# TensorE's order where phases follow each other: from the scheduler's choice to an order by counts of passed columns

## The chip, the core and the metric

The kernel runs on one NeuronCore of one Trainium2 chip. The metric is the device time of one execution in microseconds (us), as the median of several executions. A core has five engines that run their own instruction queues side by side: TensorE (PE: matmuls, with PEld for its weight loads), VectorE (DVE), ScalarE (ACT), GpSimd (POOL) and SyncE (SP, which here only issues DMAs). They meet through semaphores.

## What is computed

A decoder of two layers over 1040 tokens (16 meta tokens and 1024 real ones), 1024 features wide, in float32. Every sub-layer stands between two RMS norms:

```
def rmsnorm(x, g):                      # over the features
    return x * rsqrt(mean(x * x) + EPS) * g

def conv_ffn(x, w_up, conv_w, w_down):
    gate, val = split(causal_dwconv(x @ w_up, conv_w))
    return (silu(gate) * val) @ w_down

for l in range(2):
    hn = rmsnorm(h, g[0])
    mix = hgrn2_mixer(hn) if l == 0 else fox_mixer(hn, *shared_kv(h))
    h = h + rmsnorm(mix, g[1])
    h = h + rmsnorm(conv_ffn(rmsnorm(h, g[2])), g[3])
return h[:, 16:]
```

So at four places a product must be finished for all 1024 features before its tokens can be normalised, added to the stream, normalised again and used by the next product: after the mixer of layer 0, after its feed-forward part, after the mixer of layer 1, and after the last feed-forward part, which ends the kernel. These four places are called the **joins** here.

## The kernel before

Features lie on partitions and tokens on columns. The tokens are cut into three blocks (`BLK_A`: 356, 342, 342 columns; `BLK_B`: 342 each), and the 1024 features into eight tiles of 128 (`KT`). A float32 product is made of float32r parts, high and low: for each tile of the contracted dimension `mm3s` (line 141) issues three matmuls (lines 145, 148, 149) of 342 or 356 columns and yields the number of columns passed, 1026 or 1068. Such three matmuls are called a **pair** in this document (a pair of weight tile and input tile). `mm3` runs `mm3s` without stopping.

The program is written with a framework that has a scheduler: it places the instructions of each engine by priority (the order of the text, shifted by `tc.high_priority(offset=...)`) and by its own idea of when operands are ready, and draws all semaphores. Inside `tc.manual_schedule(engines={PE})` TensorE's instructions stay in the order of the text. Before the change this holds for the two woven stages (lines 543, 711, 1031), not for the joins.

A join is written by `overlap(blocks, work, done, then)` (line 218). `work(acc, i, sl)` makes row tile `i` of a block: four pairs into a PSUM bank, an evacuation by DVE (line 575 or 681) and `sumsq`, which squares the tile on ACT and adds the square to `acc` on POOL (lines 187, 188). Eight row tiles, 32 pairs, make a block. `done` is `post` (line 191) for the finished block:

- `rstd_of` (line 156): six small matmuls at line 164 sum `acc` over the features (called **S** here), ACT takes the root (line 169), DVE the reciprocal and a diagonal (lines 170, 175), and six matmuls at line 176 spread it over the partitions (called **R**).
- the **gain loop** over the eight tiles: a load of the residual by DMA, a multiplication (line 207) and an addition (line 208) on DVE, a store by DMA, and where another norm follows `split_gain` (ACT line 280 or 97, DVE line 281 or 98) and the squares of the new stream, added on POOL (line 188).
- a second `rstd_of` for the norm that follows (called **PS**, its sums, and **PR**, its root), whose result ACT copies into `r` (line 179). The last join has none.

`then(b)` is the next phase's first work on block `b`: at the first and third join three hidden tiles, five times eight pairs, each with a convolution on DVE and ACT (lines 607 to 614, `high_priority`); at the second the projections k, v, q (eight pairs each) and the forget logits z (`zf`, line 736, 16 matmuls) of the first head pair.

The text before the change puts S and R of a block behind the first row tile of the next block (`LAG` 1), PS and PR of the block before it just ahead of them, the last block's S and R behind the first step of `then(0)` (`LAG2` 1); the scheduler then moves TensorE's instructions as it sees fit. Tiles have few buffers: `pj` (products) 2, `pd` (statistics) 2, `po` 1, `acc` 2, `rstd` (the diagonal) 1.

Of the kernel before, what the change touches and what calls it, by code (L numbers as in the profile page):

```python
# [20 lines left out]
KT = D // P  # L21
# [9 lines left out]
BLK_A = [(0, 356), (356, 342), (698, 342)]  # L31
# [7 lines left out]

OFF, OFF_W0, OFF_W = 1000, 0, 300  # L40

LAG, LAG2 = 1, 1


AHEAD, RUSH, SLACK = 2, 2, 5000
# [10 lines left out]
def tile_yoco(ctx: ExitStack, tc: tile.TileContext, hT, gains, lbl, w_in, head_g, w_oa,  # L56
# [92 lines left out]
            PE.matmul(pt, wl, xh[:, sl], start=False, stop=(j == n - 1))  # L149
            yield (2 + (xl is not None)) * pt.shape[-1]  # L150

    def mm3(pt, pairs, sl):
        for _ in mm3s(pt, pairs, sl):
            pass

    def rstd_of(accs, r=None):


        n = accs[0].shape[-1]
        cs = [slice(c, min(c + QR, n)) for c in range(0, n, QR)]  # L160
        pt = psum("pd")
        for j, c in enumerate(cs):
            for i, acc in enumerate(accs):
                PE.matmul(pt[:c.stop - c.start, j:j + 1], acc[:, c], ones[:, :1], start=(i == 0), stop=(i == len(accs) - 1))
        q = sm.tile([P, 4], F32, tag="rq", name=nm("rq"), bufs=2)
        m = cs[-1].stop - cs[-1].start
        k = len(cs) - (m < QR)
        for rows, j in ((QR, slice(0, k)), (m, slice(k, len(cs))))[:1 + (m < QR)]:
            A.activation(q[:rows, j], pt[:rows, j], AF.Sqrt, bias=eps[:rows])
            V.reciprocal(q[:rows, j], q[:rows, j])  # L170
        dg = tmp("rstd", n)
        pr = psum("pd")[:, :n]
        for j, c in enumerate(cs):
            m = c.stop - c.start
            V.tensor_scalar(dg[:m, c], ident[:m, :m], q[:m, j:j + 1], float(D), ALU.mult, ALU.mult)
            PE.matmul(pr[:, c], ones[:m], dg[:m, c], start=True, stop=True)
        if r is None:
            return pr
        A.copy(r, pr)
# [11 lines left out]
    def post(acc, m, sl, gpost, res, keep, pre=None, more=None):  # L191


        n = sl.stop - sl.start
        r1 = rstd_of([acc])
        acc = None
        for kt in range(KT):
            mk = m[kt][:, sl]
            if more is None or kt % 4 < 2:
                rs = tmp("res", n)  # L200
            elif isinstance(more, int):
                ru = unit(more, "res") if kt % 2 == 0 else ru
                rs = ru[:, (kt % 2) * 350:][:, :n]
            else:
                rs = tmp(more[kt % 2], n)
            nc.sync.dma_start(rs, res[kt][:, sl])
            V.scalar_tensor_tensor(mk, mk, gsb[:, gpost, kt:kt + 1], r1, ALU.mult, ALU.mult)
            V.tensor_add(mk, mk, rs)  # L208
            dst = keep(kt, sl)
            nc.sync.dma_start(dst, mk[:, n - dst.shape[-1]:])  # L210
            if pre is not None:
                split_gain(pre[1][kt], mk, pre[0], kt, sl)
                acc = sumsq(acc, mk, "sq2")
        yield
        if pre is not None:
            rstd_of([acc], pre[2][:, sl])

    def overlap(blocks, work, done, then=None):


        def row_tiles(b):
            t0, n = blocks[b]
            acc = None
            for i in range(KT):
                acc = work(acc, i, slice(t0, t0 + n))
                yield
            behind.append(done(acc, slice(t0, t0 + n)))

        def some(g, k=99):
            while k and next(g, g) is not g:  # L230
                k -= 1

        behind = []
        nb = len(blocks)
        for b in range(nb):
            g = row_tiles(b)
            some(g, LAG)
            if b:
                if b > 1:
                    next(behind[b - 2], None)  # L240
                next(behind[b - 1])
            some(g)
        g = then(0) if then else iter(())
        some(g, LAG2)
        next(behind[nb - 1])
        next(behind[nb - 2], None)
        some(g)
        for b in range(1, nb):
            g = then(b) if then else iter(())
            if b == nb - 1:  # L250
                next(behind[b], None)
            some(g)

    def weave(a, wa, b, wb, lead):

# [43 lines left out]
    def norm0(i):  # L299
        sl = slice(BLK_A[i][0], BLK_A[i][0] + BLK_A[i][1])  # L300
        accs = [None, None]
        for kt in range(KT):
            accs[kt % 2] = sumsq(accs[kt % 2], x0[kt][:, sl], eng=V if i == 0 and kt % 2 else G)
        rstd_of(accs, r0[:, sl])

    w0 = [W.cols(w_in, [D])]
    take(0)
# [238 lines left out]
    def mixer_out(o, w, blocks, WW, mix, done, then):  # L546


        mx = [None] * KT

        def part(kts):
            x = []
            for kt in kts:
                *ou, src = o(kt)
                split(*(t[:, blocks[0][0]:] for t in (*ou, src)))
                x.append((WW.rows(w, kt * P), ou))
            return x

        def one():
            x = part(range(4))  # L560
            for ot in range(KT):
                mx[ot] = unit(mix[ot], f"mix{ot}")
                for t0, n in blocks:
                    pt, sl = psum("pj")[:, :n], slice(t0, t0 + n)
                    yield from mm3s(pt, [(wt(ot), ou) for wt, ou in x], sl)
                    A.copy(mx[ot][:, sl], pt)

        def two():
            x = part(range(4, 8))

            def work(acc, ot, sl):
                pt = psum("pj")[:, :sl.stop - sl.start]
                mm3(pt, [(wt(ot), ou) for wt, ou in x], sl)
                with tc.high_priority(offset=OFF):
                    V.tensor_add(mx[ot][:, sl], mx[ot][:, sl], pt)
                    return sumsq(acc, mx[ot][:, sl])

            overlap(blocks, work, lambda acc, sl: done(acc, mx, sl), then)

        return one, two  # L580
# [16 lines left out]
    def ffn(l, blocks, x, r, WW, hid, accu, done, then=None):  # L597
# [22 lines left out]
        def tile_up(j):  # L620
            c0, m = HID[j]

            ua, ub = hid[count["hid"] % len(hid)]
            hh, hl = unit(ua, f"h{j}", F32R), unit(ub, f"h{j}", F32R) if m == P else None
            count["hid"] += 1
            ws = [WW.cols(w_up[l], [c0]), WW.cols(w_up[l], [DFF + c0])] if m == P else [WW.cols(w_up[l], [c0, DFF + c0])]
            halo = [None, None]

            def block(t0, n):
                sl, y = slice(t0, t0 + n), []  # L630
                for i, w in enumerate(ws):
                    if i:
                        yield
                    pt = psum("pj")[:, :n]
                    mm3(pt, [(w(kt), x[kt]) for kt in range(KT)], sl)
                    with tc.high_priority(offset=OFF):
                        yi, halo[i] = conv(pt, j + i * FT, halo[i], sl)
                    y.append(yi)
                if m < P:
                    y.append(tmp("y", n))  # L640
                    A.copy(y[1][:m], y[0][m:2 * m])
                yg, yv = y[0][:m], y[1][:m]
                A.activation(yg, yg, AF.Silu)
                V.tensor_mul(yv, yv, yg)
                if m == P:
                    split(hh[:, sl], hl[:, sl], yv)
                else:
                    A.copy(hh[:m, sl], yv)
                    V.tensor_sub(hh[m:, sl], yv, f(hh[:m, sl]))
                yield  # L650

            return (hh, hl), block

# [18 lines left out]
        def downs(ci, hs, ws):  # L672

            def down(ot, sl):
                pt = psum("g")[:, :sl.stop - sl.start]
                mm3(pt, [(w(ot), h_) for w, h_ in zip(ws, hs)], sl)
                with tc.high_priority(offset=OFF):
                    if ci == 0:
                        A.copy(acc_u[ot][:, sl], pt)
                    else:  # L680
                        V.tensor_add(acc_u[ot][:, sl], acc_u[ot][:, sl], pt)  # L681

            def work(acc, ot, sl):
                down(ot, sl)
                with tc.high_priority(offset=OFF):
                    return sumsq(acc, acc_u[ot][:, sl])

# [3 lines left out]
            for ot in range(KT):  # L691
                if ci == 0:
                    acc_u[ot] = unit(accu[ot], f"acc{ot}")
                for t0, n in blocks:
                    down(ot, slice(t0, t0 + n))

        count = {"hid": 0, "halo": 0}
        return first, rest
# [301 lines left out]
    def heads0(i):  # L1000
# [3 lines left out]
        for which in ("zkvq" if i == NB - 1 else "kvqz"):  # L1004
            if which == "z":
                zf(i, *zs)
                forget(i, *zs)
            else:
                for _ in project(which, 0, i):
                    pass  # L1010
            yield
        if i:
            turn(0, i - 1)
        if i == NB - 1:
# [61 lines left out]
```

## Time and profile before

| | us |
|---|---|
| median of three runs | 2878.49 (2877.14 to 2882.29) |
| the profiled execution, its own time | 2883.05 |
| its span, first to last instruction | 2881.1 |
| TensorE busy / DVE busy / ACT busy / POOL busy | 2768.6 / 1830.8 / 1258.2 / 369.6 |
| TensorE's mean granted clock | 0.982 of full |

The table's engine times are sums over the span. All numbers of the trace come from the profiled execution, which is 4.6 us above the median. A granted clock of 1.00 is 2.4 GHz; the other level that the rows show is half of it, and a stretch between the two had both.

### The profile page before, as it was taken

The page shows a single profiled execution, that of the slowest core. Times are in us where ns is not written, and L with a number is a line of the kernel's source. Part 1 is how long each engine was busy: PE and PEld are TensorE (multiplying, and loading weights), DVE is VectorE, ACT ScalarE, POOL GpSimd, SP SyncE. Part 2 cuts the span into 40 slices and gives each one's busy share as a digit, 9 for nine tenths or more (in the row PEclk, how much of TensorE's full clock was granted, in tenths as well). Part 3 has the DMA queues.
Part 4 walks back from the last instruction along what each step waited for, and adds up shares of the span by engine and source line. Part 5 has one row for each costly group of instructions (what it writes and reads, how often), then busy time and mean ns, then how long its engine had stood idle before and what let it go on. Part 6 is the DMA issues. An engine that isn't in the chain of part 4 may idle for free. (4 is left out here: it accounts for less than half of the span.)

```text
span 2881.1 us, 45581 instructions
## 1 busy us (share of the span) xinstructions
PE 2768.6 (96%) x17706; PEld 2709.2 (94%) x17706; DVE 1830.8 (64%) x3737; ACT 1258.2 (44%) x2421; POOL 369.6 (13%) x741
## 2 busy tenths in 40 slices
PE   8999999989999999999889999999989999999997
PEld 8999999989999999999789988898989999999997
DVE  5545445285655655566878888887684665565566
ACT  6445445455322322233566666666555232232232
POOL 2000000041100000004400000000240100010012
PEclk9999999999999999999899999999999999999999
DMA  4111111142211111112311111112242111121103
GB/s 132 30 38 30 38 40 49 37 125 62 66 38 52 45 52 38 44 52 67 92 45 45 45 45 45 45 45 93 70 124 59 45 52 52 30 65 39 52 30 113
DMA packets 202921, 163.14 MB, mean 57 GB/s; under 512 B 13984, under 2 KB 194128, under 8 KB 202704
## 3 DMA queue, kind: packets, MB, share of 16 engines
q1 hardware_dynamic: 202704, 160.23, 19.2%
q8 instruction: 138, 2.26, 0.3%
q14 instruction: 79, 0.65, 0.1%
HBM read 139.53 MB, written 20.66 MB: 56 GB/s over the span
## 5 line engine op out<-in xcount | busy, mean ns | idle before, releaser
L145 PE MATMUL pj<-x,wh 128*128 128x342 f32 (+1 forms) x2640 | 871.1, 330 | 12.6 <-DVE u L607 6.3
L149 PE MATMUL pj<-x,wl 128*128 128x342 f32 (+1 forms) x2640 | 849.3, 322 | 2.8 <-DVE wl L98 2.8
L148 PE MATMUL pj<-x,wh 128*128 128x342 f32 (+1 forms) x2640 | 849.3, 322 | 0.0
L145 PEld LDWEIGHTS pj<-x,wh 128*128 128x128 f32 x2640 | 500.8, 190 | 18.9 <-DVE u L607 7.2
L149 PEld LDWEIGHTS pj<-x,wl 128*128 128x128 f32 x2640 | 499.9, 189 | 3.1 <-DVE wl L98 3.1
L148 PEld LDWEIGHTS pj<-x,wh 128*128 128x128 f32 x2640 | 501.5, 190 | 0.1
L145 PE MATMUL g<-h,wh 128*128 128x342 f32 (+1 forms) x1056 | 339.0, 323 | 0.3
L149 PE MATMUL g<-h,wl 128*128 128x342 f32 (+1 forms) x1056 | 337.7, 321 | 0.4 <-DVE wl L138 0.4
L148 PE MATMUL g<-h,wh 128*128 128x342 f32 (+1 forms) x1008 | 323.8, 322 | 0.0
L97 ACT CAST wh<-raw 128x1024 fp32r<-128x1024 f32 x142 | 146.0, 1045 | 341.6 <-PE g L148 282.1
L145 PE MATMUL pj<-hnh,wh 128*128 128x356 f32 (+1 forms) x720 | 261.8, 364 | 9.3 <-ACT wh L97 7.0
L681 DVE TENSOR_TENSOR acc<-acc,g 128x342 f32<-128x342 f32 (+1 forms) x288 | 147.2, 511 | 193.6 <-PE g L149 193.4
L98 DVE TENSOR_TENSOR wl<-raw,wh 128x1024 fp32r<-128x1024 f32 x142 | 180.6, 1281 | 87.1 <-ACT wh L97 76.3
L149 PE MATMUL pj<-hnh,wl 128*128 128x356 f32 (+1 forms) x720 | 233.1, 324 | 0.8 <-DVE wl L98 0.8
L148 PE MATMUL pj<-hnl,wh 128*128 128x356 f32 (+1 forms) x720 | 232.8, 323 | 0.0
L612 ACT ACTIVATE y<-u,cw 128x342 f32<-128x342 f32 (+1 forms) x258 | 150.5, 584 | 182.6 <-DVE u L607 171.9
L188 POOL TENSOR_TENSOR acc<-acc,sq 128x342 f32<-128x342 f32 (+1 forms) x162 | 168.9, 1049 | 426.5 <-ACT sq L187 396.4
L613 DVE SCALAR_TENSOR_TENSOR y<-u,cw,y 128x342 f32<-128x342 f32 (+1 forms) x258 | 148.5, 576 | 111.4 <-ACT y L612 111.2
L607 DVE TENSOR_TENSOR u<-pj,r 128x342 f32<-128x342 f32 (+1 forms) x258 | 132.2, 513 | 114.1 <-PE pj L149 110.8
L145 PEld LDWEIGHTS g<-h,wh 128*128 128x128 f32 x1056 | 198.7, 189 | 2.5 <-ACT h L97 0.6
L149 PEld LDWEIGHTS g<-h,wl 128*128 128x128 f32 x1056 | 199.4, 189 | 0.6 <-DVE wl L138 0.6
L148 PEld LDWEIGHTS g<-h,wh 128*128 128x128 f32 x1008 | 190.6, 189 | 0.7 <-DVE h L98 0.2
(237 smaller groups left out, 4937.8 us busy)
## 6 DMA issues: line engine op xcount, KB each, us to landing
raw<-in_w_up_dram SPq DMA_DIRECT2D x84, 512.0 KB, 4.0
raw<-in_w_dn_dram SPq DMA_DIRECT2D x42, 512.0 KB, 4.7
raw<-in_w_in_dram SPq DMA_DIRECT2D x32, 512.0 KB, 4.1
raw<-in_kv_w_dram SPq DMA_DIRECT2D x16, 512.0 KB, 4.1
res<-h SPq DMA_DIRECT2D x44, 171.0 KB, 2.8
h<-mix SPq DMA_DIRECT2D x40, 171.0 KB, 2.2
cn<-csum SPq DMA_DIRECT2D x32, 171.0 KB, 3.6
raw<-in_w_oa_dram SPq DMA_DIRECT2D x8, 512.0 KB, 3.5
```

Of the source, the lines that this page charges most:

```text
L97: A.copy(hi, src)
L98: V.tensor_sub(lo, src, f(hi))
L145: PE.matmul(pt, wh, xh[:, sl], start=(j == 0), stop=False)
L148: PE.matmul(pt, wh, xl[:, sl], start=False, stop=False)
L149: PE.matmul(pt, wl, xh[:, sl], start=False, stop=(j == n - 1))
L188: eng.tensor_add(acc, acc, sq)
L607: V.tensor_mul(u[:, 2:], pt, r()[:, sl])
L612: A.activation(y, u[:, 2:], AF.Copy, scale=cw[:, j, 2:3])
L613: V.scalar_tensor_tensor(y, u[:, 1:n + 1], cw[:, j, 1:2], y, ALU.mult, ALU.add)
L681: V.tensor_add(acc_u[ot][:, sl], acc_u[ot][:, sl], pt)
```

## The change

`overlap` now puts the whole join under `tc.manual_schedule` for TensorE. `work` and `then` are generators that yield the columns of each pair; `main` runs them one after the other, and a counter `at` adds up the columns. When a block's row tiles are done, its `post` is put on a list with a due count, `at + LAG_SUM`; whenever the counter passes the due count of an entry, that entry is run to its next `yield` and is due again that many columns later. `post` yields `LAG_ROOT` between S and R, `LAG_NEXT` between the gain loop and PS, and `LAG_ROOT` again between PS and PR. So S stands 6500 columns behind the block's end, R 7600 behind S, PS 31000 behind R, PR 7600 behind PS, each rounded up to whole pairs. Before `then(b)` starts, all of `post` of block `b` is run out. The root of the first norm goes to the PSUM tag `po` rather than `pd`, and the diagonal is made before the yield.

```
-LAG, LAG2 = 1, 1
+LAG_SUM, LAG_ROOT, LAG_NEXT = 6500, 7600, 31000
...
-    def mm3(pt, pairs, sl):
-        for _ in mm3s(pt, pairs, sl):
-            pass
-
-    def rstd_of(accs, r=None):
+    def rstd_of(accs, r=None, tag="pd"):
...
         dg = tmp("rstd", n)
-        pr = psum("pd")[:, :n]
         for j, c in enumerate(cs):
             m = c.stop - c.start
             V.tensor_scalar(dg[:m, c], ident[:m, :m], q[:m, j:j + 1], float(D), ALU.mult, ALU.mult)
+        yield LAG_ROOT
+        pr = psum(tag)[:, :n]
+        for j, c in enumerate(cs):
+            m = c.stop - c.start
             PE.matmul(pr[:, c], ones[:m], dg[:m, c], start=True, stop=True)
...
-        r1 = rstd_of([acc])
+        r1 = yield from rstd_of([acc], tag="po")
...
-        yield
         if pre is not None:
-            rstd_of([acc], pre[2][:, sl])
+            yield LAG_NEXT
+            yield from rstd_of([acc], pre[2][:, sl])
 
     def overlap(blocks, work, done, then=None):
...
+        def main():
+            for t0, n in blocks:
+                acc = None
+                for i in range(KT):
+                    acc = yield from work(acc, i, slice(t0, t0 + n))
+                yield done(acc, slice(t0, t0 + n))
+            for b in range(len(blocks) if then else 0):
+
+                for _ in all_behind[b]:
+                    pass
+                yield from then(b)
+
+        at, behind, all_behind = 0, [], []
+        with tc.manual_schedule(engines={mybir.EngineType.PE}):
+            for x in main():
+                if isinstance(x, int):
+                    at += x
+                else:
+                    behind.append([at + LAG_SUM, x])
+                    all_behind.append(x)
+                for y in list(behind):
+                    if y[0] <= at:
+                        k = next(y[1], None)
+                        if k is None:
+                            behind.remove(y)
+                        else:
+                            y[0] = at + k
+            for _, g in behind:
+                for _ in g:
+                    pass
...
             def work(acc, ot, sl):
                 pt = psum("pj")[:, :sl.stop - sl.start]
-                mm3(pt, [(wt(ot), ou) for wt, ou in x], sl)
+                yield from mm3s(pt, [(wt(ot), ou) for wt, ou in x], sl)
...
                 for i, w in enumerate(ws):
-                    if i:
-                        yield
                     pt = psum("pj")[:, :n]
-                    mm3(pt, [(w(kt), x[kt]) for kt in range(KT)], sl)
+                    yield from mm3s(pt, [(w(kt), x[kt]) for kt in range(KT)], sl)
...
             if which == "z":
                 zf(i, *zs)
                 forget(i, *zs)
+                yield 2 * KT * BLK_A[i][1]
             else:
-                for _ in project(which, 0, i):
-                    pass
-            yield
+                yield from project(which, 0, i)
```

## Rows read from the trace of the kernel before

**Rows 1.** Page, part 1: busy time, share of the span, instructions.
```profile
PE 2768.6 (96%) x17706; PEld 2709.2 (94%) x17706; DVE 1830.8 (64%) x3737; ACT 1258.2 (44%) x2421; POOL 369.6 (13%) x741
```
**Rows 2.** Waits of TensorE: us in total, times, longest us.
```profile
PE pd L164 <- POOL acc L188: 15.1, 12, 3.6
PE pd L176 <- DVE rstd L175: 9.7, 11, 3.1
```
**Rows 3.** Busy time by stretch: us, each engine (instructions), clock, DMA share, GB/s.
```profile
569.90:613.50 43.60, 39.90 (x228) 38.33 (x227) 30.61 (x63) 19.71 (x44) 20.96 (x21) 0.88 0.26 77
613.50:687.00 73.50, 65.20 (x403) 63.25 (x402) 65.75 (x122) 44.43 (x83) 29.83 (x46) 0.95 0.42 122
1340.10:1383.50 43.40, 39.24 (x229) 38.18 (x227) 31.93 (x64) 18.09 (x45) 22.89 (x22) 0.88 0.27 84
1383.50:1452.00 68.50, 56.47 (x313) 52.30 (x313) 55.96 (x103) 43.94 (x86) 25.16 (x20) 0.88 0.34 100
2069.00:2112.10 43.10, 39.77 (x229) 38.44 (x228) 28.91 (x63) 19.64 (x45) 20.82 (x22) 0.88 0.25 74
2112.10:2187.00 74.90, 66.53 (x422) 63.99 (x420) 67.46 (x124) 48.74 (x86) 26.65 (x47) 1.00 0.43 125
613.50:640.40 26.90, 24.88 (x154) 23.74 (x152) 26.83 (x48) 15.91 (x31) 13.66 (x19) 1.00 0.57 168
```
**Rows 4.** Line 145 alone, one matmul a pair: stretch, us, busy (matmuls), clock, DMA.
```profile
545.00:569.00 24.00, 16.08 (x50) 9.25 (x49) 1.00 0.31 88
569.90:598.00 28.10, 15.40 (x47) 8.69 (x46) 1.00 0.34 101
613.50:640.40 26.90, 15.26 (x47) 8.75 (x47) 1.00 0.57 168
613.50:666.00 52.50, 26.54 (x80) 15.52 (x80) 0.93 0.47 140
1383.50:1406.70 23.20, 9.23 (x24) 5.57 (x24) 0.85 0.58 162
```
**Rows 5.** Timeline of the first join: start, us, engine, line [idle before <- releaser].
```profile
572.16 0.78 PE L164 MATMUL pd<-ones,acc 128*128 128x1 f32 x6 [0.40 <-POOL acc L188]
575.93 0.59 PE L176 MATMUL pd<-rstd,ones 128*128 128x128 f32 x4
598.06 1.20 PE L164 MATMUL pd<-ones,acc 128*128 128x1 f32 x6 [2.42 <-POOL acc L188]
609.01 1.05 DVE L207 SCALAR_TENSOR_TENSOR mix<-mix,gsb,pd 128x342 f32<-128x342 f32 x2 [1.72 <-PE pd L176]
617.86 0.76 PE L164 MATMUL pd<-ones,acc 128*128 128x1 f32 x6 [0.23 <-POOL acc L188]
630.70 0.68 PE L176 MATMUL pd<-rstd,ones 128*128 128x128 f32 x4 [0.32 <-DVE rstd L175]
640.41 0.76 PE L164 MATMUL pd<-ones,acc 128*128 128x1 f32 x6 [1.17 <-POOL acc L188]
650.45 0.73 PE L176 MATMUL pd<-rstd,ones 86*128 86x86 f32 x2 [3.07 <-DVE rstd L175]
```
**Rows 6.** Line 208 in the first gain loop and the last: ns min/median/max.
```profile
L208 DVE TENSOR_TENSOR mix<-mix,res x8: 519/1278/1292, 578.0 to 594.7; 128x356 f32<-128x356 f32 x8
L208 DVE TENSOR_TENSOR acc<-acc,res x4: 507/507/515, 2870.2 to 2875.9; 128x342 f32<-128x342 f32 x4
```
**Rows 7.** DVE's groups in 613.5 to 640.4 and 631.4 to 658: busy us, mean ns.
```profile
L98 DVE TENSOR_TENSOR wl<-raw,wh 128x1024 fp32r<-128x1024 f32 x4 | 5.9, 1514 | 0.0
L208 DVE TENSOR_TENSOR mix<-mix,res 128x342 f32<-128x342 f32 x11 | 5.6, 522 | 0.8 <-DMA res<-in_hT_dram 0.7
```
**Rows 8.** TensorE's timeline at the other joins: start, us, line [idle before <- releaser].
```profile
1367.01 1.35 PE L164 MATMUL pd<-ones,acc 128*128 128x1 f32 x6 [3.63 <-POOL acc L188]
1419.84 0.40 PE L145 MATMUL pj<-x,wh 128*128 128x342 f32 x1 [4.19 <-DVE z L743]
2096.48 1.12 PE L164 MATMUL pd<-ones,acc 128*128 128x1 f32 x6 [2.57 <-POOL acc L188]
```

More of the change, by code (lines that the diff above doesn't have):

```diff
@@ L213, in post @@
                 acc = sumsq(acc, mk, "sq2")
-        yield
         if pre is not None:
-            rstd_of([acc], pre[2][:, sl])
+            yield LAG_NEXT
+            yield from rstd_of([acc], pre[2][:, sl])
     def overlap(blocks, work, done, then=None):
[L221 to L225, printed above, removed]
-                yield
[L227 to L252, printed above, removed]
+        def main():
[26 more added lines that the diff above has]
+                    pass
     def weave(a, wa, b, wb, lead):
@@ L303, in norm0 @@
             accs[kt % 2] = sumsq(accs[kt % 2], x0[kt][:, sl], eng=V if i == 0 and kt % 2 else G)
-        rstd_of(accs, r0[:, sl])
+        for _ in rstd_of(accs, r0[:, sl]):
+            pass
     w0 = [W.cols(w_in, [D])]
@@ L649, in block @@
                     V.tensor_sub(hh[m:, sl], yv, f(hh[:m, sl]))
-                yield
             return (hh, hl), block
@@ L675, in down @@
                 pt = psum("g")[:, :sl.stop - sl.start]
-                mm3(pt, [(w(ot), h_) for w, h_ in zip(ws, hs)], sl)
+                yield from mm3s(pt, [(w(ot), h_) for w, h_ in zip(ws, hs)], sl)
                 with tc.high_priority(offset=OFF):
@@ L683, in work @@
             def work(acc, ot, sl):
-                down(ot, sl)
+                yield from down(ot, sl)
                 with tc.high_priority(offset=OFF):
@@ L694, in downs @@
                 for t0, n in blocks:
-                    down(ot, slice(t0, t0 + n))
+                    for _ in down(ot, slice(t0, t0 + n)):
+                        pass
         count = {"hid": 0, "halo": 0}
@@ L1007, in heads0 @@
                 forget(i, *zs)
+                yield 2 * KT * BLK_A[i][1]
             else:
-                for _ in project(which, 0, i):
-                    pass
-            yield
+                yield from project(which, 0, i)
         if i:
```

## The prediction, made before the changed kernel was run

> **What bounds the kernel now.** I read the page first: TensorE is busy for 96% of the span, so only its idle and its slow time can be won [rows 1]. Then who it waits for: the two statistics lines alone stand for 15.1 and 9.7 us [rows 2]. Third, the joins by stretch [rows 3]: a block's end to the end of the row tiles, then the next phase's first work. Last, TensorE's timeline there [rows 5, 8].
>
> The unit is the pair: 50 in 24.0 us at full clock, 0.48 us each [rows 4]; a statistic takes 0.75 us [rows 5]. In a first part 64 pairs and six statistics are 64 x 0.48 + 6 x 0.75 = 35.2 us; the rows have 43.6, 43.4 and 43.1, so about 8 us are lost in each [rows 3]. In the second part of join 1 the 403 matmuls less 36 of statistics are 122 pairs, 63.1 us with six statistics, of 73.5: 10.4 lost. Join 3, likewise: 422 - 36 is 129 pairs, 66.4 of 74.9: 8.5 lost. Join 2: 313 matmuls less 36, at 0.16 us (a third of a pair), are 44.3 and 4.5 for statistics, 48.8 of 68.5: 19.7 lost [rows 3]. In all some 63 us, of idle time and of half clock (granted 0.88 in the first parts).
>
> The reader should see a second thing: **DVE**. From 613.5 to 640.4 it is busy for 26.83 of 26.90 us [rows 3]. There TensorE isn't late because its order is poor; it waits for an engine without a gap.
>
> **The change, part by part.** By the code, counts become pairs: 6500 columns are 7 pairs, 7600 are 8, 31000 are 31 (of 1026). At 0.48 us a pair S stands 3.4 us behind a block's end, R 3.8 behind S, PS 14.9 behind R, PR 3.8 behind PS.
>
> *S and R.* The first S now waits 0.40 at 572.16, 2.3 us after the block's end [rows 5]; at 3.4 us that wait is gone: -0.4 a join, and as much for each of the two earlier blocks of join 4, -0.8. R follows S by 3.1 us there (572.9 to 576), so 3.8 cover it. If POOL or DVE are behind, the cover is gone: at 617.86 S opens 4.3 us after the tiles' end (613.5) [rows 5], 0.9 later than it will be asked for.
>
> *PS of block 0.* Its gain loop starts at R's end, 6.6 us after the block's end (576.5), and opens PS 28.2 us after it (598.06) [rows 5]; joins 2 and 3: 26.9 and 27.5 [rows 3, 8]. TensorE asked 2.42, 3.63 and 2.57 us before. Now PS stands at pair 7 + 8 + 31 = 46; join 1 had 47 ahead of it [rows 4]: the same place, with S of block 1 in front instead of behind. The loop, however, starts at 15 x 0.48 + 2 x 0.75 = 8.7 us, 2.1 later. Less 0.5 because the row tiles that share DVE stop when TensorE does, PS waits 4.0, 5.2 and 4.2 us: +1.6 a join. The half clock behind it was there before too. With the 0.4 won by S, a first part gets **1.2 us longer** (bounds 0 and 3).
>
> What is won: R of block 1 stands one pair behind PS, so its loop starts some 12 us before the tiles' end instead of 4.5 (609.01) [rows 5].
>
> *PS of blocks 1 and 2 in joins 1 and 3* decide. PS of block 1 now stands behind 47 pairs of the next phase [rows 4]. By the counts R of block 1 is at pair 47 behind block 0, PS at 78, the tiles end at 64: 14 pairs into the next phase, **33 pairs or 16 us earlier**. PS of block 2 moves from 80 [rows 4] to 15 + 31 = 46. TensorE's queue is in order: everything behind PS waits, and with it the products that feed DVE's convolutions.
>
> When does it open? TensorE arrives at 14 x 0.48 + 0.75 + 0.9 = 8.4 us. The loop has had 12 us at the pace of block 0's, eight L208 in 17 us (578.0 to 594.7) [rows 6]: some five tiles. Ahead of the other three DVE has three weight splits at 1.5 us [rows 7], the last evacuations and one convolution (3 us); the three tiles cost some 3.5 and square and POOL addition behind them 2: 13 us. It waits 4.5 (0 if the loop comes first, 8 if DVE puts all convolution work first). R of block 2 follows a pair later, behind a reciprocal on a full DVE: 0.5.
>
> PS of block 2: from R (631.4) to the end of that loop now takes 26.5 us, of which three L208 out of eleven and what goes with them belong to block 1 [rows 7], 3.5 us. So 23 us, against 31 pairs and PR: 15.6, or 18.6 with slow time in it. It waits 4 (0 to 8).
>
> Each such stall is as long as those that now bring half clock [rows 5, 8]. Join 1's second part has one spell: clock 0.95 of 73.5 us, 3.7 us lost [rows 3], part of it idle: I take 3 behind each stall (0 to 4.5). Together 0.9 + 4.5 + 3 + 0.5 + 4 + 3 = 15.9 us, in place of 10.4 in join 1 and 8.5 in join 3: **+5.5 and +7.4**.
>
> *Join 2.* PS of block 1 moves from 24 pairs [rows 4] to 14, PS of block 2 hardly: 24 + 24 against 46. I take a wait of 4.2 and 3 us of half clock at the first, R 0.5, the k weights 1.8 as now; the wait for z (4.19 [rows 8]) stays at 3.5 with 3 of half clock, since z's evacuation still lies behind block 2's loop on DVE; 0.9 for roots: 16.9 in place of 19.7, **-2.8** (bounds -12 and +5).
>
> *Edits without a price of their own.* No matmul, DMA or evacuation is added. `po` has one buffer; R of a block needs it after the loop before has read its last tile, some 3 us earlier by the loops above; its next user is the attention, behind all of it: 0. The diagonal has one buffer: PR's waits for R, a pair behind PS, 3 us ahead of PR: 0 (up to 1 each). `acc` has two: a new block's first square waits for the S before it, at pair 7 rather than 4; the other squares queue behind it on ACT, and the POOL additions catch up over eight tiles: 0 (up to 0.5). The scheduler can no longer put other ready matmuls into a wait; that is in the waits above. SP keeps its order of loads and stores, issued by the same loops.
>
> *The rule that speaks against the change.* L208 takes 1.28 us in block 0's loop, beside POOL's additions, and 0.51 in the last, with POOL free [rows 6]. The Trainium skill (SBUF — State Buffer, section "Who interferes with whom") says that a DVE instruction with two SBUF inputs and a GpSimd instruction that reads SBUF shut each other out for a whole instruction; the trace agrees, 1.28 against 0.51. By that rule a loop that is moved among row tiles costs DVE up to 8 x 0.77 = 6.2 us more; without it PS of block 0 would open in time.
>
> **The sum.** Join 1: 1.2 + 5.5 = 6.7; join 2: 1.2 - 2.8 = -1.6; join 3: 1.2 + 7.4 = 8.6; join 4: -0.8. Together +12.9 us on the profiled execution's 2883.05: 2896. That execution is 4.6 above the median, so **2891 us**. About 0.2% (6 us) is what a measurement here can tell from no change.
>
> **The rivals.**
> (a) *Faster: the loops keep up.* Block 1's loop starts 7 us earlier and the row of S, R, PS, PR at half clock behind 598 goes. If the loops then need no more than the 15 to 16 us between R and PS, nothing waits at PS; that is the point from which it decides. Of the 63 lost us, some 13 in join 2 (weights and z) and two or three evacuation waits a join don't depend on it; half of the other 50 gives 2853, all of it 2828. For it: the last loop's L208 at 0.51 [rows 6], DVE's idle 13 us in the first part [rows 3]. Against: block 0's loop took 20 to 21.5 us with nothing but row tiles beside it.
> (b) *No change*: PS waits two or three us each; what is won in R and half clock is lost there: 2873 to 2884.
> (c) *Much slower*: DVE's fixed order puts convolutions and splits first, PS waits its 8 us twice in joins 1 and 3, each with 4.5 of half clock: 16 more a join than now, 2912.
> (d) *The counts aren't kept*: a stalled TensorE passes no columns, so after the stall at block 0 the later counts come later in time. If that stall (4 to 5 us) and its half clock carry PS of blocks 1 and 2 past their loops' ends, each of joins 1 and 3 is left with one stall: 8 us less a join than forecast, 2875.
>
> **Chances and range.** My forecast with (c), slower by over 0.2%: 0.55; (b) and (d), within it, 0.18; (a) 0.27. The range leaves 1 in 10 out on either side: down to half of the losses gone, 2853; up to (c), 2912. Both signs hold weight; the forecast's own range is 2884 to 2905.
>
> **What would show it.** Right: PE idle before L164, longest 4 to 5 us, some 26 to 30 us after the first block's end, and again 8 and 30 us into joins 1 and 3's next phase, with POOL's additions named; line 164's total above 15.1 us; L176's below 9.7; clock 0.9 or less in those second parts, and first parts no shorter than 43 us. Wrong: no wait over 1 us before L164, second parts near 63 and 66 us; then DVE had more room than its full stretch shows. If weights (L97, L98) or `pj` evacuations (L607) top the list of waits instead, the stall has only changed its name.

## The result, and the profile after

The changed kernel takes **2911.7 us** (median; 2910.2 to 2913.6) against 2878.4 of the kernel before in the same comparison: a ratio of 1.0114, 95% interval 1.0096 to 1.0131, 33 us slower. Forecast were 2891 us, 13 us slower. The sign and the place were right; the size was two and a half times the sum. The time lies outside the forecast's own range, 2884 to 2905, and at the upper end of the whole one, 2853 to 2912.

The line numbers of the changed kernel: S and PS are line 161, R and PR line 176, the loop's multiplication and addition 207 and 208. Its waits of TensorE (us in total, times, longest us), to be held against [rows 2]:

```profile
PE pd L161 <- POOL acc L188: 45.1, 11, 8.9
PE pd L161 <- POOL u L609: 23.0, 2, 11.5
PE pd L176 <- DVE rstd L171: 3.6, 3, 2.3
```

TensorE's busy time stands still (2767.5 us for 2768.6 [rows 1]); the sums alone now wait 68.1 us for 15.7 (the 15.1 of [rows 2] and 0.6 behind line 609), and the roots' matmuls wait for their diagonal 4.6 (1.0 of it into `po`) for 9.7. The stretches of joins 1 to 3, first and second part each, in the columns of [rows 3]:

```profile
569.50:613.20 43.70, 38.11 (x230) 37.55 (x229) 32.64 (x67) 21.63 (x47) 23.81 (x23) 0.88 0.31 91
613.20:701.40 88.20, 66.69 (x398) 65.83 (x397) 65.83 (x118) 45.72 (x81) 26.89 (x43) 0.86 0.33 94
1355.10:1398.70 43.60, 37.75 (x230) 37.20 (x229) 33.02 (x67) 20.75 (x48) 23.12 (x23) 0.88 0.30 89
1398.70:1467.20 68.50, 54.33 (x314) 51.89 (x313) 52.71 (x99) 43.89 (x84) 23.50 (x19) 0.88 0.32 96
2080.90:2123.50 42.60, 36.96 (x230) 36.11 (x229) 32.52 (x66) 20.25 (x46) 23.26 (x23) 0.92 0.30 87
2123.50:2210.80 87.30, 68.05 (x398) 67.22 (x397) 64.65 (x118) 44.08 (x80) 26.67 (x44) 0.84 0.34 97
```

Against [rows 3]: join 1 takes 131.9 us for 117.1, join 2 112.1 for 111.9, join 3 129.9 for 118.0. Before, join 3's second part held 422 matmuls against 398 now: 24 of later work, 8 pairs or 3.8 us, had slipped in there, so that the like-for-like loss is 15.7 us. The span grew by 27.3 (2881.1 to 2908.4): +14.8, +0.2, +15.7, and, with those 8 pairs counted in the rest both times, 3.4 less there. (Between the medians it is 33, since the profiled execution before lay 4.6 us above its median and the one after 1.5 below.)

TensorE in join 1, and below in join 3 (start, us, line [idle before <- releaser]):

```profile
599.20 1.35 PE L161 MATMUL pd<-ones,acc 128*128 128x1 f32 x6 [5.52 <-POOL acc L188]
601.40 1.41 PE L176 MATMUL po<-rstd,ones 128*128 128x128 f32 x6
617.91 0.76 PE L161 MATMUL pd<-ones,acc 128*128 128x1 f32 x6 [1.12 <-POOL acc L188]
633.21 1.30 PE L161 MATMUL pd<-ones,acc 128*128 128x1 f32 x6 [11.49 <-POOL u L609]
636.30 1.38 PE L176 MATMUL po<-rstd,ones 128*128 128x128 f32 x6
661.85 1.31 PE L161 MATMUL pd<-ones,acc 128*128 128x1 f32 x6 [8.89 <-POOL acc L188]
...
2145.50 1.31 PE L161 MATMUL pd<-ones,acc 128*128 128x1 f32 x6 [11.52 <-POOL u L609]
2147.67 1.41 PE L176 MATMUL po<-rstd,ones 128*128 128x128 f32 x6
2172.72 1.30 PE L161 MATMUL pd<-ones,acc 128*128 128x1 f32 x6 [6.47 <-POOL acc L188]
```

From the top: PS of block 0, R of block 1, S of block 2, PS of block 1, R of block 2, PS of block 2. The reader should see the order in the middle: R of block 2, on which the third gain loop starts, stands right **behind** the PS that waits 11.5 us. (The "u" of line 609 is a small fill that POOL ran just behind the last addition; the addition, 632.24 to 633.16, is what opened PS.)

### The profile page after: what moved, and what is told of

The parts are those of the page before. It is cut to its first block, busy times and chain, and to the rows that moved or that the text cites. A ratio compares the mean times of both kernels' runs of the same rounds, so it can differ in the third digit from the quotient of the medians.

```text
span 2908.4 us, 45577 instructions
## 1 busy us (share of the span) xinstructions
PE 2767.5 (95%) x17706; PEld 2715.9 (93%) x17706; DVE 1831.2 (63%) x3737; ACT 1262.0 (43%) x2422; POOL 371.0 (13%) x741
```

## The experiments

Every ratio is against the kernel before, with its 95% interval.

**Is it only the place?** e1 gives PS a place of its own for each block; e2 one later place for all.

```
-LAG_SUM, LAG_ROOT, LAG_NEXT = 6500, 7600, 31000
+LAG_SUM, LAG_ROOT = 6500, 7600
+NEXT_UP, NEXT_QKV = [41000, 48000, 57000], [41000, 38000, 35000]
...
-            yield LAG_NEXT
+            yield (NEXT_QKV if gpost == 3 else NEXT_UP)[sl.start // 349]
```

> One number of the change moved: the sums PS stand later, by block (41, 47 and 56 pairs behind R in joins 1 and 3; 41, 37 and 35 in join 2) and all else as in the changed kernel (31 pairs). Theory P (the place of PS is what costs): the eight waits at PS, 61 us in the changed kernel, fall below 15 us in total, spells of half clock behind them go, and the time falls to 2840 to 2865, below the kernel before, because S, R and PS then stand better than the scheduler had them. Rival O (the fixed order as such costs, since ready matmuls can no longer fill a wait): the waits move to other places and the time stays above 2880.

```
-LAG_SUM, LAG_ROOT, LAG_NEXT = 6500, 7600, 31000
+LAG_SUM, LAG_ROOT, LAG_NEXT = 6500, 7600, 41000
```

> The count between R and PS is 41000 columns instead of 31000, 10 pairs or 4.8 us later everywhere. Theory P: each wait at PS shrinks by 4.8 us or to nothing, from 61 to some 23 us, with two or three half-clock spells fewer: 2865 (2858 to 2875). Rival O: within 8 us of the changed kernel's 2912.

e1: 2906.7 us, 1.0094 (1.0079 to 1.0109); e2: 2909.2 us, 1.0101 (1.0084 to 1.0118). The place alone gives almost nothing, so theory P fell; what its rival O said of the time came true, but e5 below shows that a fixed order as such isn't the cost. The waits of e1, whose sums are line 162 and whose roots' matmuls line 177:

```profile
PE pd L177 <- DVE rstd L172: 62.3, 9, 16.8
PE po L177 <- DVE rstd L172: 10.7, 8, 3.4
PE pd L162 <- POOL acc L189: 5.2, 3, 4.0
```

The sums now wait 5.2 us, the roots' matmuls 73.0: the stall has changed its name. One chain shows why, on TensorE, ScalarE and VectorE (start, us):

```profile
605.00 0.68 PE L162 MATMUL pd<-ones,acc 128*128 128x1 f32 x6
607.40 0.39 ACT L167 ACTIVATE rq<-pd,eps 128x2 f32<-128x2 f32 x2
618.23 0.50 DVE L209 TENSOR_TENSOR mix<-mix,res 128x342 f32<-128x342 f32 x1
619.14 0.21 DVE L168 RECIPROCAL rq<-rq 128x2 f32<-128x2 f32 x2
619.87 1.32 DVE L172 TENSOR_SCALAR rstd<-ident,rq 128x128 f32<-128x128 f32 x3
620.30 1.69 PE L177 MATMUL pd<-rstd,ones 128*128 128x128 f32 x6 [10.77 <-DVE rstd L172]
```

The root is ready at 607.8, its reciprocal of 0.21 us runs at 619.14, among the last additions (line 209) of block 1's gain loop. TensorE's order is the order of the text, so a later PS is also a later text for the instructions that it issues on the other engines: at 31000 columns PS stood one pair ahead of the next block's loop in the text, at 41000 behind it, and the scheduler goes by the text where nothing shifts a priority.

**The statistic's chain first.** e5 is e1 with the three instructions put first; e6 and e7 put the same lines into the changed kernel and the kernel before.

```
+            with tc.high_priority(offset=OFF):
                 A.activation(q[:rows, j], pt[:rows, j], AF.Sqrt, bias=eps[:rows])
                 V.reciprocal(q[:rows, j], q[:rows, j])
...
+            with tc.high_priority(offset=OFF):
                 V.tensor_scalar(dg[:m, c], ident[:m, :m], q[:m, j:j + 1], float(D), ALU.mult, ALU.mult)
```

> The later places of e1, and with them the scheduler is told to put a statistic's square root (ScalarE), reciprocal and diagonal (VectorE) ahead of the other work of their engines. Theory Q (in e1 the wait only moved from the sums of the second norm to its root's matmul, because the reciprocal and the diagonal stood in VectorE's queue behind the whole gain loop of the next block): the waits at the root's matmul, 73 us in the trace of e1, fall below 20 us, those at the sums stay near 5 us, and the time falls to 2850 to 2875 us. Theory D (VectorE has too much work in the joins whatever stands first): the waits come back at the sums or at the first matmuls of the next block, and the time stays at 2890 us or more.

> The changed kernel with its places as they are, and only the square root, the reciprocal and the diagonal of a statistic put ahead of the other work of ScalarE and VectorE. Theory Q: the waits of the changed kernel are at the sums of the second norm (68 us of gaps), which wait for the gain loop and not for a root; the root's matmul waits 3.6 us in all, so that no more than some 5 us come back: 2903 to 2912 us. Rival: the loops themselves are held up by roots that come late (the loop of the second block starts on a root's matmul), and then the time falls below 2895 us.

> The kernel before, with the square root, reciprocal and diagonal of a statistic put ahead of the other work of their engines. Its waits at the root's matmul are 9.7 us in all. Theory Q: about half of that comes back, 2870 to 2878 us. Rival: the scheduler already gave the order of these instructions by when their inputs come, and nothing changes beyond 2 us.

e5: 2859.7 us, **0.9939 (0.9915 to 0.9962)**. e6: 2914.1, 1.0123 (1.0105 to 1.0141), no better than the changed kernel. e7: 2880.6, 1.0005 (0.9994 to 1.0017): its rival held, nothing comes back. So neither edit is worth anything alone (the place 5 us against the changed kernel, the order nothing), and both together are worth 52. These four runs show it.

> The same kernel as e5, timed in more rounds beside the next one: 2855 to 2864 us.

2860.2 us, 0.9936 (0.9922 to 0.9950). This kernel beats both. Its waits, two stretches and its chain in join 1 (sums line 162, roots' matmuls line 179):

```profile
PE po L179 <- DVE mix L210: 12.0, 3, 5.1
PE pd L162 <- POOL acc L191: 7.8, 6, 3.3
PE po L179 <- DVE acc L210: 7.2, 2, 4.4
```

```profile
569.50:606.60 37.10, 34.84 (x232) 34.31 (x231) 31.02 (x65) 21.15 (x45) 23.61 (x23) 1.00 0.33 98
606.60:679.40 72.80, 65.08 (x399) 63.46 (x399) 65.76 (x120) 44.10 (x82) 27.61 (x45) 0.95 0.42 119
```

```profile
601.04 0.68 PE L162 MATMUL pd<-ones,acc 128*128 128x1 f32 x6
602.05 0.32 DVE L169 RECIPROCAL rq<-rq 128x2 f32<-128x2 f32 x2
605.44 0.81 PE L179 MATMUL pd<-rstd,ones 128*128 128x128 f32 x6
...
620.38 1.58 PE L179 MATMUL po<-rstd,ones 128*128 128x128 f32 x6 [5.08 <-DVE mix L210]
```

The reciprocal now runs 1 us behind the sums, with no wait before 605.44. The first part fell from 43.6 to 37.1 us at full clock, next to the 35.2 that its pairs and statistics need; the second, 72.8, is hardly shorter than before. What is late next is R, which waits until the loop before it has read `po` for the last time (`po` has one buffer).

**Whose chain, and is R's new wait pure loss?** e9 puts only the second norm's chain first; e8 is e5 with R later.

```
-            with tc.high_priority(offset=OFF):
+            with tc.high_priority(offset=OFF if r is not None else 0):
```

> The later places of e1, with the square root, reciprocal and diagonal put first for the second norm's statistic alone; those of the first norm keep their place. Theory Q: all of the gain of e5 over e1 (47 us) hangs on the second norm's chain behind the next gain loop, and the time is that of e5, 2855 to 2866 us. Rival: the first norm's chain, behind which a gain loop starts, carries a part of it (in e1 the waits at its matmul into po are 10.7 us, 8 of them), and the time is 2870 us or more.

```
+ROOT_UP, ROOT_QKV = [7600, 12600, 18600], [7600, 10600, 12000]
-NEXT_UP, NEXT_QKV = [41000, 48000, 57000], [41000, 38000, 35000]
+NEXT_UP, NEXT_QKV = [41000, 43000, 46000], [41000, 36000, 31000]
...
-        yield LAG_ROOT
+        yield lag
...
```

> e5 with the root's matmul of the first norm asked for later in blocks 1 and 2 (by 5 and 11 thousand columns in joins 1 and 3, by 3 and 4 thousand in join 2), and the second norm's sums about where they were. In e5 that matmul waits 17.6 us in all (five times, longest 5.1) until the loop of the block before has read its last tile out of the only buffer of po. Theory B: the loop could not start earlier anyhow, so the wait is TensorE's loss alone, and passing columns in it gives 8 to 18 us back: 2842 to 2852 us. Rival: the loops then start some us later than now, the second norm's sums and the next phase's first products wait for them, and the time stays within 4 us of e5 or rises.

e9: 2872.0 us, 0.9975 (0.9965 to 0.9985). Theory Q, all of the gain, fell: 35 of the 47 us between e1 and e5 come with the second norm's chain, and the other 12 when the first's is added (the first's alone was not run). e8: 2863.5 us, 0.9946 (0.9934 to 0.9959): the rival held. R's waits fell from 19.2 to 8.0 us, those of the sums rose from 7.8 to 24.1. The wait for the loop was moved along TensorE's queue, not removed there.

**What makes the loop late?** In joins 1 to 3, e3 loads the residual for the first tile of a block alone, e4 has ScalarE write the low part as a second copy.

```
+            if pre is not None and kt:
+                pass
...
-            nc.sync.dma_start(rs, res[kt][:, sl])
+            if pre is None or not kt:
+                nc.sync.dma_start(rs, res[kt][:, sl])
```

> In joins 1 to 3 the residual is loaded for the first of the eight tiles of a block only and that load is added to all eight: seven loads a block are left out, DVE, ACT, POOL and TensorE do the same work. Theory L (PS of blocks 1 and 2 opens late because the gain loop hangs on its residual loads, two buffers, issued in order on SP behind stores and weight loads): waits at PS of block 1 in joins 1 and 3 fall from 11.5 to 4 to 6 us, of block 2 from 8.9 and 6.5 to below 5, block 0's stay at 5; time 2885 to 2895. Theory D (they open late because DVE is full): the waits stay within 1.5 us, time 2905 to 2915.

```
-                split_gain(pre[1][kt], mk, pre[0], kt, sl)
+                for x in pre[1][kt]:
+                    if pre[0] is None:
+                        A.copy(x[:, sl], mk)
+                    else:
+                        A.mul(x[:, sl], mk, gsb[:, pre[0], kt:kt + 1])
```

> In the gain loops of joins 1 to 3 the low part of the split is written by ScalarE (a second scaled copy, not the remainder) instead of VectorE: VectorE has 8 instructions of 0.58 us less a block, 4 us. Theory D: each wait at PS shrinks by 3 to 4 us, block 1's from 11.5 to 8, time 2875 to 2890. Theory L: block 0's wait shrinks from 5.5 to 2 or 3 (there DVE is full), those of blocks 1 and 2 in joins 1 and 3 stay within 1.5 us; time 2895 to 2905.

e3: 2899.2 us, 1.0066 (1.0051 to 1.0081); e4: 2892.3 us, 1.0043 (1.0031 to 1.0056). Both leave work out and serve for timing alone. What they save, 12.5 and 19.4 us, is nearly what the sums wait less: 54.6 and 48.1 us for 68.1. Block 1's R and PS, e3 in join 1, then e4 in joins 1 and 3:

```profile
602.88 1.41 PE L176 MATMUL po<-rstd,ones 128*128 128x128 f32 x6
631.87 1.31 PE L161 MATMUL pd<-ones,acc 128*128 128x1 f32 x6 [7.77 <-POOL u L612]
```

```profile
598.25 0.80 PE L176 MATMUL po<-rstd,ones 128*128 128x128 f32 x6
630.79 1.31 PE L161 MATMUL pd<-ones,acc 128*128 128x1 f32 x6 [13.44 <-POOL u L613]
2102.30 1.41 PE L176 MATMUL po<-rstd,ones 128*128 128x128 f32 x6
2129.79 1.31 PE L161 MATMUL pd<-ones,acc 128*128 128x1 f32 x6 [7.33 <-POOL u L613]
```

From R to PS, in us (e4 has 4.6 us less on VectorE, eight low parts at 0.58):

| | changed kernel | e3, loads left out | e4, low part moved |
|---|---|---|---|
| block 1, joins 1 and 3 | 31.8, 32.5 | 29.0, 28.6 | 32.5, 27.5 |
| block 2, joins 1 and 3 | 25.6, 25.1 | 21.8, 20.9 | 23.6, 21.7 |

So the loads count in every one of these loops; the low part counts in all but block 1's of join 1, where the wait even grew (13.4 us for 11.5). PS of block 0 waits 3.0, 0 and 2.9 us in e4's three joins, where the changed kernel has 5.5, 5.4 and 4.9; e3 leaves it where it was. Neither theory holds for all loops.

**Does one wait make the other?** e10 is e6 with PS two pairs later, meant to stand behind the next block's R.

```
-LAG_SUM, LAG_ROOT, LAG_NEXT = 6500, 7600, 31000
+LAG_SUM, LAG_ROOT, LAG_NEXT = 6500, 7600, 33200
```

> The changed kernel with its statistic's root, reciprocal and diagonal put first, as in e6 (2914 us), and one number besides: the second norm's sums two pairs (1 us) later, 33200 columns behind the root for 31000, so that they stand behind the root's matmul of the next block and no longer one pair ahead of it. Theory H (what makes the changed kernel slow is above all that the waiting sums hold back the matmul on which the next gain loop starts, so that the second wait is made by the first): the sums of block 2 wait under 3 us instead of 8.6 and 6.6, those of block 1 some 4 us less in joins 1 and 3, and the time falls to 2875 to 2895 us. Rival E (the place is too early by far more than a pair, whatever stands behind it): 2905 to 2915 us.

2894.4 us, 1.0058 (1.0040 to 1.0076). The rounding to whole pairs gave the new order for R of block 2 in join 3 but not in joins 1 and 2, so one run holds both cases (R of block 1 went ahead of PS of block 0 in all three). Join 1, then join 3:

```profile
631.47 1.30 PE L161 MATMUL pd<-ones,acc 128*128 128x1 f32 x6 [10.73 <-POOL u L611]
632.64 1.56 PE L178 MATMUL po<-rstd,ones 128*128 128x128 f32 x6
...
2133.16 0.90 PE L178 MATMUL po<-rstd,ones 128*128 128x128 f32 x6 [0.17 <-DVE mix L209]
2144.18 1.30 PE L161 MATMUL pd<-ones,acc 128*128 128x1 f32 x6 [9.61 <-POOL acc L190]
2162.94 0.66 PE L161 MATMUL pd<-ones,acc 128*128 128x1 f32 x6
```

Where R went first (2133.16), the next PS, at 2162.94, waits for nothing, for 6.6 us in e6; where it stayed behind in join 1, the next PS still waits 6.4 us, at 658.2. So in join 3 the second wait is made by the first. (In join 2 R of block 2 stands behind a wait of 11.7 us, and the next PS waits for nothing, as in the changed kernel: one wait need not make another.) The wait at PS of block 1 is not cured by it (10.7 and 9.6): it comes from the early place, and in e5b, 48000 columns behind R, it is gone. Theory H has the time right, but of its waits only block 2's in join 3; besides, PS of block 0 waits 1.6, 0.4 and 4.0 us, where the changed kernel has 5.5, 5.4 and 4.9.

## Why the prediction was right in sign and short in size

*What held.* S of block 0 in join 1 no longer waits; S of block 2 waits 1.12 us (forecast 0.9); R's waits fell below 9.7 as said. PS of block 0 waits 5.5, 5.4 and 4.9 (4.0, 5.2, 4.2). TensorE reaches PS of block 1 in join 1 at 633.21 - 11.49 = 621.7, 8.5 us after the tiles' end (8.4). Join 2, with +0.2 for -1.6, and join 4, unchanged for -0.8, are near. In join 4 the two waits of 0.4 are gone as forecast, but the last S waits 3.5 for 2.4. Join 2 is near by luck: PS of block 1 waits 6.9 us for 4.2 there, and z 1.0 for 3.5. First parts came out at +0.1, +0.2 and -0.5 where 1.2 was taken, within the bounds 0 and 3 bar the last, and by luck too: by the stretches TensorE's idle time grew by 1.9, 1.7 and 2.3 us, and its busy time, for as many matmuls (230 for 228 or 229), fell by 1.8, 1.5 and 2.8, because less of it ran at half clock, which the forecast had left as it was.

*The step that failed: when PS of block 1 opens.* I had 13 us after the tiles' end: 7.5 for splits, evacuations and a convolution, 3.5 for three tiles, 2 for square and addition. It opened after 20.0. The splits and the loop's last additions in the changed kernel (VectorE), all engines in the stretch between those additions (columns of [rows 3]), and SP's queue beside them:

```profile
613.58 1.96 DVE L99 TENSOR_TENSOR wl<-raw,wh 128x1024 fp32r<-128x1024 f32 x1
615.88 3.06 DVE L99 TENSOR_TENSOR wl<-raw,wh 128x1024 fp32r<-128x1024 f32 x2
620.46 0.50 DVE L208 TENSOR_TENSOR mix<-mix,res 128x342 f32<-128x342 f32 x1
623.51 0.50 DVE L208 TENSOR_TENSOR mix<-mix,res 128x342 f32<-128x342 f32 x1
627.47 0.51 DVE L208 TENSOR_TENSOR mix<-mix,res 128x342 f32<-128x342 f32 x1
630.65 0.52 DVE L208 TENSOR_TENSOR mix<-mix,res 128x342 f32<-128x342 f32 x1 [1.45 <-DMA res<-in_hT_dram]
```

```profile
620.46:630.65 10.19, 1.25 (x8) 0.96 (x6) 8.27 (x18) 5.96 (x10) 3.33 (x4) 0.67 0.73 209
```

```profile
628.01 0.33 SPq L210 DMA_DIRECT2D h<-mix  x1
628.38 0.92 SPq L206 DMA_DIRECT2D res<-in_hT_dram  x2
```

The splits were priced well: 613.2 to 620.46 is 7.3 us. The tail is 2.6, from 630.65 to 633.21. Between them lie three steps from tile to tile of 3.4 us each, **10.2 us where 3.5 was written**. I had priced a tile at 1.2 us; the row for block 0's loop, which I had cited for the first five tiles, showed 17 us over seven steps, 2.4 each [rows 6]. Here the three tiles' own nine instructions take 5.3 us added up; eight of other work stand between them with 4.1 (two steps of a convolution 1.8, a weight split 1.2, reciprocals and diagonal of block 2's first norm 1.1), all overlapping a little; and VectorE is idle for 1.9, of which 1.45 before 630.65 go to a load. SP's queue, in order, puts that load (628.38) behind the store of the tile just added.

Four tiles were left instead of three, too, as the loop started 9 us ahead of the tiles' end (604.2) and not 12. By the prediction's own counts 17 pairs and PR lie between R of block 1 and the tiles' end, 8.9 us at full clock: the 12 has no sum behind it.

What each part is worth the runs settle only in part. In join 1 leaving the loads out shortens the whole loop by 2.8 us and moving the low part does nothing; in join 3 they give 3.8 and 5.0. The convolutions and the weight split between the tiles were not taken away in any run.

*PS of block 2* waits 8.9 and 6.5 us for 4. From R to PS the loop takes 25.6 and 25.1 us (636.30 to 661.85, 2147.67 to 2172.72) for 23; TensorE was there after 16.7 and 18.6, for 15.6 or 18.6. That the first wait makes the second was in the working, as R "a pair later"; e10 shows it alone, in join 3.

*Half clock was priced too high.* Join 1's second part loses 88.2 less 362/3 x 0.48 and 4.5, 25.8 us, for 15.9 forecast. Idle before line 161 are 1.1 + 11.5 + 8.9 = 21.5; 4.3 remain for half clock and all else, where 6.5 stood. So of the 9.9 us that the forecast was short in this part, PS of block 1 accounts for 7.0, PS of block 2 for 4.9, S for 0.2, and 2.2 go the other way. Likewise join 3: 24.9 lost, 19.3 idle, 5.6 the rest.

*The rivals.* (b) fell: the waits at PS are 5 to 12 us, not two or three. (c) gave the time, 2912, by another road: its waits of 8 twice are 11.5 with 8.9 or 6.5, its cause, VectorE's fixed order, was not told apart from the pace from tile to tile, and its extra half clock wasn't there. (a), that loops which keep up free the first parts, is what e5 does, and it names the price nearly (2853 for 2860), though by taking half of what is lost; but its point, a loop of 15 to 16 us, is never reached: a place had to be found that leaves some 23 to 35 us, together with another order on VectorE. That second condition, that a moved PS moves its reciprocal in the text too, is in none of my rivals. (d) didn't happen.

*The rule on the shared port.* The changed kernel's addition takes 0.50 us at 640.20 and 1.24 at 646.06, in one loop; an addition of POOL runs beside the second (645.76 to 646.92), and POOL is idle beside the first. The Trainium skill (SBUF — State Buffer, section "Who interferes with whom") says that a VectorE instruction with two SBUF inputs, as this one, and a GpSimd instruction that reads SBUF shut each other out. With that the trace agrees, though no run here took POOL's additions out of a loop to price it.

## What to carry to other kernels

Fix one engine's order by hand, and you set through the text the order of everything that a moved step issues elsewhere: look at the short instructions of its chain (here 0.21 and 1.3 us on VectorE) and put them first, or the wait only moves from one line to the next. Price a loop by the distance from step to step that a row of the same loop shows, not by what its instructions are busy. And a step that may wait should not stand ahead of the one on which the next loop starts: in join 3 one wait made the next.

## What the runs showed of the hardware

Three waits show what a stall can do to the clock. R in e5's second timing stands behind an idle time of 2.2 us at 596.5 and takes 0.87, and behind one of 5.1 at 620.38 and takes 1.58. In the kernel before, PS of block 0 stands behind 2.42 us at 598.06 and takes 1.20, where S takes 0.76 to 0.78 [rows 5]. The stretches behind the three, in the columns of [rows 3], e5's two first:

```profile
596.50:600.50 4.00, 3.98 (x27) 4.00 (x28) 4.00 (x7) 2.15 (x6) 2.75 (x4) 1.00 0.64 183
620.30:626.00 5.70, 5.62 (x22) 5.62 (x23) 5.17 (x12) 2.75 (x6) 2.10 (x5) 0.54 0.68 197
```

```profile
598.00:613.50 15.50, 15.44 (x75) 15.25 (x76) 8.48 (x22) 5.54 (x14) 4.66 (x6) 0.67 0.11 33
```

Behind the wait of 2.2 us TensorE kept 2.4 GHz; behind that of 5.1 it ran nearly all of the 5.7 us at 1.2; and behind that of 2.42, hardly longer than the first, the mean over 15.5 us is 0.67, with TensorE busy throughout. So a short wait is not always free, and these rows don't say what sets the two short ones apart.

ScalarE reloads its function table for 1.28 us each time the root and the gate's function take turns; between 656 and 672 in the changed kernel it did so five times, 6.4 of 16 us, one of them just ahead of a root that was due.
